# Tying hand-ordered operations of a decoder-layer kernel to one another, with weight splits behind bank copies in two attentions

## The chip, the cores and the metric

The kernel runs on one core of a Trainium2 chip. The metric is the device time in microseconds (us) of one execution; the time of a kernel is the median of its runs.

## The reference, cut to what matters

One decoder layer, in fp32: sequence length 1024, model width 1024, feed-forward width 2816, 256 memory tokens.

```python
def reference(x, mem, ...):
    h = rms_norm(x, norm1_g)
    p_rwkv, p_sb, q_mem, gate_logits = jnp.split(h @ w_in, cut, axis=-1)
    y_a = rwkv7_branch(p_rwkv, ...)                 # 8 heads of 64, a recurrence over time
    y_b = stick_breaking_branch(p_sb, ...)          # 8 heads of 64, causal, QK-norm
    y_m = memory_branch(q_mem, mem, ...)            # 4 heads of 128 into 256 memory tokens
    gates = jax.nn.sigmoid(gate_logits.reshape(b, t, 3, 1024))
    branch_out = jnp.einsum('btnc,ncd->btnd', jnp.stack([y_a, y_b, y_m], 2), w_branch)
    x = x + jnp.sum(gates * branch_out, axis=2) @ w_out
    return x + conv_ffn(rms_norm(x, norm2_g), w_up, conv_w, conv_b, w_down)

def stick_breaking_attention(q, k, v):              # by blocks of 128 queries
    z = q @ k.T * scale
    log_1mb = jnp.where(mask, log_sigmoid(-z), 0.0)
    log_between = reverse_cumsum(log_1mb) - log_1mb
    return jnp.where(mask, jnp.exp(log_sigmoid(z) + log_between), 0.0) @ v
```

## The kernel before

**Arithmetic.** A large fp32 product is done as three products on numbers that are split into a high part and a low part: high by high, high by low, low by high (`mm3`). A weight tile of 128x1024 is loaded through SyncE's DMA queue (`load_w`, L77) into one of two raw buffers and split by `split_raw`: ScalarE writes the high part (L81), then GpSimd the low part, raw minus high (L82). Each of the two has two buffers. `mmul` (L113) issues every product, `transpose` (L106) every transpose, both on TensorE.

**Banks.** The accumulators are eight PSUM banks of 128x512: four named `mm`, for the projections, and four named `g`, for all the rest. A projection piece needs two `mm` banks, which the function that ends it (`fin`) copies out: L755 for a branch gate (the sigmoid comes later, in `close`), L777 for the keys and L806 for the queries of stick-breaking, all on ScalarE; L1035 and L1036 on ScalarE and L1037 on VectorE for the memory's queries.

**Stages, in the order of the source.** (1) Startup. (2) `rwkv_prep`, four head pairs. (3) `sb_attn`, stick-breaking: 64 units, each of one head and 128 queries; a unit makes scores with a sigmoid, a scan on VectorE (L854), transposes with copies on ScalarE (`mid`, L866; the sigmoid is L848), and products with the values. (4) `mem_attn`, eight units. (5) `stage2`, the recurrence over 16 chunks, with ScalarE copies L538 and L550 and a VectorE update L530 in each; `norm_part` brings the group norm's squares (L580) between the chunks. (6) `group_norm`. (7) `branch_last` and `out_proj`. (8) `up_phase`, in steps that end in a convolution; its last operation writes the tile `gall`. (9) `down_phase`: per step two operands are split, ScalarE's L1676 and L1677 and VectorE's L1678 and GpSimd's L1679 (`prep`), and early in it the weights' sums are made (`t_sums`, L1655 and L1656). At the end of each pair of the up projection `act_sums` adds four tiles on VectorE (L1490).

**Two streams.** Projections run as a list of items, each a generator cut into pieces (eight per projection, one per 128 rows of the input); `pump` steps through them. `weave(main, pump, ratio)` takes one step of a stage and then `ratio` pieces of projection. In `sb_attn` the ratio is 1.03, in `mem_attn` 1.6, in `stage2` 2.08. `need(name)` runs pieces until an item has set the mark `name`: a head pair's queries and keys (`sb0` to `sb3`), the memory's keys and values (`kv`), a memory head's queries. The items beside stick-breaking are its later keys and queries with gates, then the memory's keys and values (`mv` and `mk`, eight short items of two or three pieces), then the memory's queries. `load_y` (L1118 loads, L1129 is its split on ScalarE) and `branch_item` (L1165 stores partial sums to `mrd`) run beside the recurrence.

**Who sets the order.** Instructions are written down in the order of the source, and a scheduler then orders each engine's queue by priority and its own estimate of when operands are ready, so that an operation may be moved ahead of one written earlier. `self.pinned(ins)` fixes an operation, while `self.pin` is set (from the end of startup to the group norm's end, in `branch_last`, for the last tile of the output projection, in the up projection and from the fourth step of the down projection): `keep_in_program_order` puts it behind the operation that was written immediately before it on the same engine, fixed or not. If that one slips, the fixed one may slip with it, past operations that were fixed earlier. Products, transposes and the attentions' copies and scans are fixed; the weight split (L81, L82) and the bank copies L755, L777 and L806 are not.

Of the kernel before, what the change touches and what calls it, by code (L numbers as in the profile page):

```python
# [12 lines left out]
F32 = mybir.dt.float32  # L13
F32R = mybir.dt.float32r
BF16 = mybir.dt.bfloat16
AF = mybir.ActivationFunctionType
ALU = mybir.AluOpType
# [33 lines left out]
class Trunk:  # L51
    def __init__(self, ctx, tc, I, out):
        self.ctx, self.tc, self.nc, self.I, self.out = ctx, tc, tc.nc, I, out
        self.uid = 0
        self.pin = False

    def nm(self, s):
        self.uid += 1
# [19 lines left out]
        return raw  # L78

    def split_raw(self, raw, hi, lo):  # L80
        self.nc.scalar.activation(hi, raw, AF.Copy)  # L81
        self.nc.gpsimd.tensor_tensor(lo, raw, hi.bitcast(F32), ALU.subtract)  # L82
        return hi, lo

    def split_w(self, src):
# [22 lines left out]
    def pinned(self, ins):  # L108
        if self.pin:
            self.tc.keep_in_program_order(ins)  # L110

    def mmul(self, *a, **k):
        self.pinned(self.nc.tensor.matmul(*a, **k))  # L113
# [635 lines left out]
    def gate_item(self, b, d, hook={}, keep=None):  # L749
        nc = self.nc  # L750

        def fin(pp):
            g = self.t4()
            for h in range(2):
                nc.scalar.activation(g[:, h * 512 : (h + 1) * 512], pp[h], AF.Copy)  # L755
            nc.vector.tensor_tensor(g, g, self.rbc, ALU.mult)  # L756

            def close():
                self.pinned(nc.scalar.activation(g, g, AF.Sigmoid))
                if keep is None:  # L760
                    nc.scalar.dma_start(self.gsd[b, d], g)
                else:
                    keep["g", d] = g

            self.open_gates.append(close)

        return self.proj_item(self.I["w_in"][30 + b * 8 + d], fin, hook)

    def sb_qk(self, p, out):
        nc = self.nc  # L770
        st = {}
        lo64, hi64 = slice(0, 64), slice(64, 128)

        def k_fin(pp):
            kr, sq = self.t4(), self.t4()
            for h in range(2):
                nc.scalar.activation(kr[:, h * 512 : (h + 1) * 512], pp[h], AF.Copy)  # L777
            nc.scalar.activation(sq, kr, AF.Square)
            st["k"] = sq, kr

        def k_ss():
            st["ex"] = self.expand_heads(self.head_norm(self.head_ss(st["k"][0]), 2, SBD, 1.0))

        def k_bc():
            kr = st["k"][1]
            bc = self.bcast_heads(st["ex"])
            for h in range(2):
                hs = slice(h * 512, (h + 1) * 512)
                nc.vector.scalar_tensor_tensor(kr[:, hs], kr[:, hs], self.par("sbk"), bc[h], ALU.mult, ALU.mult)
            st["K"] = [], []  # L790

        def k_split(i):
            kr = st["k"][1]
            K, KL = st["K"]
            for x in (K, KL):
                x.append(self.t4("qk", F32R))
            q, o = (lo64, hi64) if i == 0 else (hi64, lo64)
            nc.scalar.activation(K[i][q], kr[q], AF.Copy)
            nc.scalar.activation(K[i][o], kr[q], AF.Copy)
            nc.vector.tensor_tensor(KL[i][q], kr[q], K[i][q].bitcast(F32), ALU.subtract)  # L800
            nc.vector.tensor_tensor(KL[i][o], kr[q], K[i][q].bitcast(F32), ALU.subtract)

        def q_fin(pp):
            qr, sq = self.t4(), self.t4()
            for h in range(2):
                nc.scalar.activation(qr[:, h * 512 : (h + 1) * 512], pp[h], AF.Copy)  # L806
            nc.scalar.activation(sq, qr, AF.Square)
            st["q"] = sq, qr

        def q_split(i):  # L810
            qr = st["q"][1]
            st.setdefault("S", []).append(self.t4("qk", F32R))
            S = st["S"][i]
            q, o = (lo64, hi64) if i == 0 else (hi64, lo64)
            g = self.par("sbq")[q]
            nc.scalar.activation(S[q], qr[q], AF.Copy, scale=g)
            nc.vector.scalar_tensor_tensor(S[o], qr[q], g, S[q].bitcast(F32), ALU.mult, ALU.subtract)  # L817
            if i == 1:
                out.extend((st["S"], *st["K"], st["f"]))

        def q_ss():
            nf = self.small("nf", [128, 16])
            st["f"] = self.head_norm(self.head_ss(st["q"][0]), 2, SBD, SBD ** -0.5, nf)

        w = self.I["w_in"]
        hooks = {1: lambda: k_split(1), 3: q_ss, 4: lambda: q_split(0), 6: lambda: q_split(1)}
        kq = {4: k_bc, 5: lambda: k_split(0)}
        return self.proj_item(w[18 + p], k_fin), k_ss, self.proj_item(w[14 + p], q_fin, kq), hooks

    def sb_attn(self, qk, need):  # L830
# [952 lines left out]
    def run(self):  # L1783
        nc, tc = self.nc, self.tc
# [44 lines left out]
        def pumped():  # L1829
            due = 0  # L1830
            for _ in self.stream(items):
                due += pace[0]
                while due >= 10:
                    due -= 10
                    next(inv, None)
                yield

        pump = pumped()

        def need(name):  # L1840
            while name not in marks:
                next(pump)
# [2 lines left out]
            self.weave(self.rwkv_prep(p, krv[p], need), pump, 1.0)  # L1845
        pace[0] = 8
        need("sb0")
        self.weave(self.sb_attn(qk, need), pump, 1.03, 0)
        need("kv")
        self.weave(self.mem_attn(mq, need), pump, 1.6, 0)  # L1850
        need("mem")
        st2 = self.stage2()
        next(st2)
        need("y1")
# [83 lines left out]
```

## Time and profile before

| | |
|---|---|
| runs | 1835.12, 1835.45, 1835.46 us; median 1835.45 us |
| profiled execution | 1834.23 us, its span from first to last instruction 1832.5 us |
| mean granted TensorE clock | 0.997 |
| TensorE busy | 1783.7 us of the span |
| stick-breaking, 334 to 648 us | TensorE 308.36, VectorE 252.89, ScalarE 189.05, GpSimd 90.18 us busy |
| memory attention, 689 to 767 us | TensorE 76.82, VectorE 31.18, ScalarE 44.80, GpSimd 17.80 us busy |
| recurrence, 810 to 1014 us | TensorE 196.94 us busy, clock 0.98 |
| up projection, 1190 to 1613 us | TensorE 416.61, VectorE 323.01 us busy |
| down projection, 1613 to 1832 us | TensorE 211.38, VectorE 153.01 us busy |

All these are of one profiled execution, the runs apart. A busy time counts instructions under way on that engine. In rows of the timeline the columns are start, duration, engine, line, operation, output and inputs with their shapes, how many instructions the row holds, and in brackets the idle time before it and what ended that. In rows of the waits: who waited, for whom, total, times, longest. In rows of the windows: from and to, length, then the busy time and number of instructions of TensorE, its weight loads, VectorE, ScalarE and GpSimd, the granted TensorE clock as a share of full speed, the share of the DMA engines and GB/s. PE is TensorE, DVE is VectorE, ACT ScalarE, POOL GpSimd, SP SyncE.

### The profile page before, as it was taken

What the parts mean: (1) busy time and instruction counts of PE and PEld (TensorE: products, weight loads), DVE (VectorE), ACT (ScalarE), POOL (GpSimd) and SP (SyncE); (2) the same over time, 40 slices, a digit from 0 to 9 for tenths busy, and PEclk for the clock granted to TensorE, in tenths of its full rate; (3) what the DMA queues carried; (4) which work ended last, traced back from release to release, by engine and by line L of the source; (5) the groups of instructions that cost most, each with busy time, mean ns of one, the idle gap of its engine ahead of it and who ended that gap; (6) DMA issues with size and microseconds to landing.
All of it is one profiled execution on the core that took longest, in us unless ns stands there. A gap on an engine that the chain in (4) does not pass through costs nothing.

```text
span 1832.5 us, 27438 instructions
## 1 busy us (share of the span) xinstructions
PE 1783.7 (97%) x10468; PEld 1442.8 (79%) x10468; DVE 1185.4 (65%) x1659; ACT 881.4 (48%) x1665; POOL 770.6 (42%) x441
## 2 busy tenths in 40 slices
PE   8999999999999999999899999989999999999999
PEld 6777778778788887787777878868888888878877
DVE  5657664988987514333534792597776777794596
ACT  5443342564666636534456533454444444444333
POOL 2322343232222452122233350476767767635454
PEclk9999999999999999999999999999999999999999
DMA  4155466111112342467665563323332323395475
GB/s 181 58 172 184 161 195 198 50 41 52 56 50 81 111 143 55 167 212 256 229 230 185 194 220 104 127 68 106 113 106 87 119 95 116 115 334 206 138 248 189
DMA packets 120614, 263.39 MB, mean 144 GB/s; under 512 B 28314, under 2 KB 40858, under 8 KB 120355
## 3 DMA queue, kind: packets, MB, share of 16 engines
q1 hardware_dynamic: 82722, 194.76, 32.3%
q10 hardware_dynamic: 33984, 54.27, 8.1%
q0 software_dynamic: 3776, 12.62, 2.2%
q8 instruction: 82, 1.34, 0.3%
q14 instruction: 50, 0.40, 0.1%
HBM read 180.04 MB, written 81.53 MB: 143 GB/s over the span
## 4 chain that ended last, share of the span: by engine, by line
PE 81%; DVE 10%; issue 4%; ACT 2%; POOL 2%; DMA 1%; ACTq 0%; SPq 0%; DVEq 0%; POOLq 0%
PE mm L113 65%; PE g L113 13%; PE g L106 3%; POOL dw L1679 1%; DVE at L854 1%; DVE it L462 1%; DVE qk L379 1%; DVE qk L381 1%; DVE inst L464 1%; DVE BT L1318 1%; DVE mg L1232 0%; DVE qk L817 0%; DMA at<-scr 0%; DVE g L1474 0%; ACT wh L81 0%
## 5 line engine op out<-in xcount | busy, mean ns | idle before, releaser
L82 POOL TENSOR_TENSOR wl<-wr,wh 128x1024 fp32r<-128x1024 f32 x77 | 196.5, 2552 | 475.0 <-ACT wh L81 464.1
L113 PE MATMUL mm<-xhi,wh 128*128 128x512 f32 x784 | 263.3, 416 | 10.1 <-ACT xhi L182 8.1
L113 PE MATMUL mm<-xlo,wh 128*128 128x512 f32 x784 | 244.7, 393 | 0.3 <-DVE xlo L183 0.3
L113 PE MATMUL mm<-xhi,wl 128*128 128x512 f32 x784 | 243.2, 392 | 0.7 <-POOL wl L82 0.7
L113 PEld LDWEIGHTS mm<-xhi,wl 128*128 128x128 f32 x784 | 147.6, 188 | 34.3 <-POOL wl L82 1.6
L113 PEld LDWEIGHTS mm<-xlo,wh 128*128 128x128 f32 x784 | 147.9, 189 | 33.8 <-DVE xlo L183 1.0
L113 PEld LDWEIGHTS mm<-xhi,wh 128*128 128x128 f32 x784 | 137.2, 190 | 40.1 <-issue 9.1
L81 ACT ACTIVATE wh<-wr 128x1024 fp32r<-128x1024 f32 x77 | 81.4, 1057 | 143.6 <-PE mm L113 87.3
L113 PE MATMUL mm<-dw,da 128*128 128x512 f32 x528 | 121.5, 390 | 2.2 <-DVE da L1678 2.0
L113 PEld LDWEIGHTS mm<-dw,da 128*128 128x128 f32 x528 | 98.8, 188 | 24.3 <-DVE da L1678 3.4
L113 PE MATMUL mm<-BT,l 128*128 128x512 f32 x504 | 117.7, 389 | 0.0
L1679 POOL TENSOR_TENSOR dw<-draw,dw 128x512 fp32r<-128x512 f32 x55 | 81.5, 1488 | 83.3 <-ACT dw L1677 83.2
L113 PE MATMUL mm<-BT,wh 128*128 128x512 f32 x352 | 109.2, 390 | 2.8 <-DVE BT L1318 2.8
L854 DVE TENSOR_TENSOR_SCAN at<-at,at 128x128 f32<-128x128 f32 (+3 forms) x64 | 93.3, 1459 | 26.6 <-ACT at L848 26.4
L113 PEld LDWEIGHTS mm<-BT,l 128*128 128x128 f32 x504 | 94.6, 188 | 19.6
L113 PE MATMUL mm<-B,wh 128*128 128x512 f32 x352 | 108.6, 390 | 1.5 <-DVE p L1508 1.5
L1678 DVE TENSOR_TENSOR da<-draw,da 128x512 fp32r<-128x512 f32 x77 | 65.7, 863 | 57.6 <-ACT da L1676 57.1
L113 PE MATMUL g<-dw,da 128*128 128x512 f32 x396 | 90.9, 390 | 2.1 <-POOL dw L1679 1.1
L1409 POOL TENSOR_TENSOR l<-it,l 128x1024 fp32r<-128x1024 f32 x21 | 51.6, 2459 | 95.5 <-ACT l L1408 95.5
L113 PEld LDWEIGHTS g<-dw,da 128*128 128x128 f32 x396 | 74.2, 188 | 18.3 <-ACT dw L1677 1.4
L1676 ACT ACTIVATE da<-draw 128x512 fp32r<-128x512 f32 x77 | 48.3, 629 | 83.6 <-PE mm L113 38.1
L756 DVE TENSOR_TENSOR w<-w,rbc 128x1024 f32<-128x1024 f32 x24 | 49.8, 2074 | 56.8 <-ACT w L755 55.0
(329 smaller groups left out, 3989.9 us busy)
## 6 DMA issues: line engine op xcount, KB each, us to landing
wr<-in_w_in_dram SPq DMA_DIRECT2D x50, 512.0 KB, 3.7
draw<-actd SPq DMA_DIRECT2D x77, 256.0 KB, 4.3
at<-scr SPq DMA_DIRECT2D x28, 512.0 KB, 6.1
draw<-in_w_down_dram SPq DMA_DIRECT2D x55, 256.0 KB, 4.9
rw<-in_w_up_dram SPq DMA_DIRECT2D x22, 512.0 KB, 3.5
actd<-gall ACTq DMA_DIRECT2D x44, 256.0 KB, 3.4
gsd<-w ACTq DMA_DIRECT2D x20, 512.0 KB, 2.8
wr<-in_w_up_dram SPq DMA_DIRECT2D x20, 512.0 KB, 3.7
```

Source lines behind the costliest of these rows:

```text
L81: self.nc.scalar.activation(hi, raw, AF.Copy)
L82: self.nc.gpsimd.tensor_tensor(lo, raw, hi.bitcast(F32), ALU.subtract)
L106: self.pinned(self.nc.tensor.transpose(out, in_, self.ident[:n, :n]))
L113: self.pinned(self.nc.tensor.matmul(*a, **k))
L379: nc.vector.tensor_tensor(bk4[q, :, first ^ h2], self.c8(x[q, hs]), self.c8(Q[q, hs]), ALU.mult)
L381: nc.vector.scalar_tensor_tensor(ra4[:, :, 1, 1:64], self.c8(P[:, hs])[:, :, 0:63], -1.0, self.c8(kk[:, hs])[:, :, 1:64], ALU.mult, ALU.mult)
L756: nc.vector.tensor_tensor(g, g, self.rbc, ALU.mult)
L854: self.pinned(nc.vector.tensor_tensor_scan(sn[:, :W][:, ::-1], sn[:, :W][:, ::-1], self.smask[:, 1024 - W :][:, ::-1], 1.0, ALU.mult, ALU. ...
L1409: keep(eng.tensor_tensor(lo, src, hi.bitcast(F32), ALU.subtract))
L1676: self.pinned(nc.scalar.activation(A[:, 0], a, AF.Copy))
L1678: self.pinned(nc.vector.tensor_tensor(A[:, 1], a, A[:, 0].bitcast(F32), ALU.subtract))
L1679: nc.gpsimd.tensor_tensor(Wt[:, 1], w, Wt[:, 0].bitcast(F32), ALU.subtract)
```

## The change

Four edits. First, `pinned` now also ties an operation to the last one that was fixed on the same engine, wherever that was (`last_pinned` is kept for the whole kernel and is never reset); the tie is an order in the queue, without a semaphore. Second, the bank copies L755, L777 and L806 are fixed. Third, a flag `pin_split` fixes both halves of the weight split, and it is set from the start of `sb_attn` to the end of `mem_attn`. Fourth, three pieces of projection run ahead of `sb_attn`, after the first head pair's mark is set; the list of items stays the same, and both versions are through the same pieces when `sb_attn` ends.

```diff
     def __init__(self, ctx, tc, I, out):
-        self.pin = False
+        self.pin = self.pin_split = False
+        self.last_pinned = {}
...
     def split_raw(self, raw, hi, lo):
-        self.nc.scalar.activation(hi, raw, AF.Copy)
-        self.nc.gpsimd.tensor_tensor(lo, raw, hi.bitcast(F32), ALU.subtract)
+        keep = self.pinned if self.pin_split else lambda ins: None
+        keep(self.nc.scalar.activation(hi, raw, AF.Copy))
+        keep(self.nc.gpsimd.tensor_tensor(lo, raw, hi.bitcast(F32), ALU.subtract))
         return hi, lo
...
     def pinned(self, ins):
         if self.pin:
             self.tc.keep_in_program_order(ins)
+            last = self.last_pinned.get(ins.ins.engine)
+            if last:
+                self.tc.add_manual_dep(
+                    ins.ins, last, mybir.DependencyInfo(mybir.DependencyClass.NoSync, mybir.DependencyReason.DATA), reason="order")
+            self.last_pinned[ins.ins.engine] = ins.ins.name
+        return ins
...
         def fin(pp):                        # gate_item; k_fin and q_fin of sb_qk likewise
-                nc.scalar.activation(g[:, h * 512 : (h + 1) * 512], pp[h], AF.Copy)
+                self.pinned(nc.scalar.activation(g[:, h * 512 : (h + 1) * 512], pp[h], AF.Copy))
...
         need("sb0")
+        self.pin_split = True
+        for _ in range(3):
+            next(pump)
         self.weave(self.sb_attn(qk, need), pump, 1.03, 0)
         need("kv")
         self.weave(self.mem_attn(mq, need), pump, 1.6, 0)
         need("mem")
+        self.pin_split = False
         st2 = self.stage2()
```

More of the change, by code (lines that the diff above doesn't have):

```diff
@@ L776, in k_fin @@
             for h in range(2):
-                nc.scalar.activation(kr[:, h * 512 : (h + 1) * 512], pp[h], AF.Copy)
+                self.pinned(nc.scalar.activation(kr[:, h * 512 : (h + 1) * 512], pp[h], AF.Copy))
             nc.scalar.activation(sq, kr, AF.Square)
@@ L805, in q_fin @@
             for h in range(2):
-                nc.scalar.activation(qr[:, h * 512 : (h + 1) * 512], pp[h], AF.Copy)
+                self.pinned(nc.scalar.activation(qr[:, h * 512 : (h + 1) * 512], pp[h], AF.Copy))
             nc.scalar.activation(sq, qr, AF.Square)
```

## The prediction

> **What bounds the kernel.** I read the page first, its busy times and the chain; then the waits, restricted to TensorE from 310 to 1020 us; then the timeline of each engine at the places where TensorE waits; last the windows, for the granted clock.
>
> ```profile
> PE 1783.7 (97%) x10468; PEld 1442.8 (79%) x10468; DVE 1185.4 (65%) x1659; ACT 881.4 (48%) x1665; POOL 770.6 (42%) x441
> ```
>
> TensorE is busy for 1783.7 of 1832.5 us. The change gives it no product less and no product more: it changes the order in which three engines are served and when three pieces of projection run. So it can move only the 48.8 us in which TensorE stands still, plus the time that it runs at a lower clock after standing still. The waits of both attentions and of the recurrence behind them, longest in total first (columns: who waited for whom, total us, times, longest):
>
> ```profile
> PE g L113 <- DVE ys L530: 3.8, 2, 3.0
> PE g L113 <- ACT qk L550: 3.3, 3, 1.8
> PE g L106 <- DVE at L854: 2.2, 2, 1.5
> PE mm L113 <- DVE qk L1037: 1.2, 1, 1.2
> PE g L106 <- DVE hn L701: 1.1, 1, 1.1
> PE g L113 <- DVE hn L701: 0.9, 1, 0.9
> PE mm L113 <- ACT w L755: 0.8, 1, 0.8
> PE mm L113 <- ACT w L806: 0.7, 1, 0.7
> ```
>
> These are all the waits of that stretch, 14 us. L530 and L550 belong to the recurrence, the other six (6.9 us) to the two attentions. The six are the most that the part of the change named in its title can win.
>
> **Part a: three pieces ahead of stick-breaking.**
>
> ```profile
> 343.44 0.33 PE L106 MATMUL g<-kon,at 128*128 128x128 f32 x1 [1.52 <-DVE at L854]
> ```
> ```profile
> 345.85 3.34 PE mm L113 x18
> ```
>
> The first unit's transposes wait 1.52 us for its scan (L854), which hangs on the queries' factors and not on TensorE. Three pieces are 18 products of 512 columns; the chain shows 18 in 3.34 us. Put ahead of the first unit they fill the 1.52 us and more: **-1.5**. They are taken from pieces that had to be run in a burst when the second head pair's mark was not yet set, so later the order of pieces and units is the same within a step. Between 0 and -1.5; I take the end, since 3.34 is over twice the wait.
>
> **Part b: weight splits behind the bank copies.**
>
> ```profile
> 387.92 1.06 ACT L81 ACTIVATE wh<-wr 128x1024 fp32r<-128x1024 f32 x1 [0.25 <-issue]
> 388.88 1.06 ACT L806 ACTIVATE w<-mm 128x512 f32<-128x512 f32 x2
> ```
>
> The split's first half (L81, 1.06 us) runs on ScalarE ahead of the two copies that empty the projection's banks (L806), and TensorE's next product waits 0.7 for such a bank. The wait of 0.8 on L755 and that of 1.2 on L1037 (the memory queries' banks) have the same L81 ahead of the same kind of copy. With the copies first each copy is ready 1.06 earlier: the 0.8 and all but 0.1 of the 1.2 go. The 0.7 goes too, but what is late next lies close:
>
> ```profile
> 390.00:400.00 10.00, 10.00 (x87) 8.13 (x86) 9.94 (x7) 7.38 (x14) 2.13 (x1) 1.00 0.25 67
> ```
> ```profile
> 402.26 1.19 PE L113 MATMUL g<-qk,qk 128*128 128x512 f32 x4 [0.86 <-DVE hn L701]
> ```
>
> VectorE is busy for 9.94 of these 10 us, and 12 us later TensorE waits for it anyway. A TensorE that is 0.7 earlier waits 0.5 longer there, so I count 0.2 of it. Together **-2.1**, between 0 (all swallowed) and -2.7.
>
> **Part c: what the later splits cost.** A fixed split stands behind whatever the source has ahead of it on ScalarE, the attention's copies too. In the long items (48 products) a split has many us to spare; in the eight short ones of the memory's keys and values it has not:
>
> ```profile
> 631.72 1.07 ACT L81 ACTIVATE wh<-wr 128x1024 fp32r<-128x1024 f32 x1 [0.46 <-issue]
> 632.69 1.24 ACT L848 ACTIVATE at<-g,nf 128x512 f32<-128x512 f32 x2
> 633.83 0.87 ACT L866 ACTIVATE at<-g 128x512 f32<-128x512 f32 x2
> ```
> ```profile
> 632.88 2.39 POOL L82 TENSOR_TENSOR wl<-wr,wh 128x1024 fp32r<-128x1024 f32 x1 [2.06 <-ACT wh L81]
> ```
> ```profile
> 637.93 0.28 PE L113 MATMUL mm<-qk,wl 128*128 128x256 f32 x1
> ```
>
> L848 and L866 are written ahead of this L81. Behind them it starts at 634.70 at the earliest instead of 631.72, 2.98 later; the GpSimd half (L82) ends at 638.25 instead of 635.27, and the first product that reads it stands at 637.93: late by 0.3. Queued behind the fixed split are later attention copies, but its own input is there, so it holds them for its 1.07 us alone. On SyncE the next weight load (L77) waits for L82 and goes 3 us later, with one item to spare. Four of eight at 0.3: **+1.2**, from 0 to +2.4 (all eight). Nothing below 0, since no product waits less for a later split.
>
> **Part d: the tie on ScalarE in the recurrence.** The tie puts every fixed operation behind the fixed one before it, in the whole kernel. Before, an operation was fixed only behind its immediate predecessor, so it could slip with it past earlier fixed ones.
>
> ```profile
> 871.48 0.33 PE L113 MATMUL g<-ys,at 64*64 64x64 f32 x4 [1.76 <-ACT qk L550]
> 872.63 0.33 PE L113 MATMUL g<-ys,at 64*64 64x64 f32 x4 [0.81 <-ACT qk L550]
> ```
> ```profile
> 871.00:877.00 6.00, 4.70 (x33) 3.79 (x34) 2.03 (x6) 1.83 (x11) 2.93 (x1) 0.72 0.65 233
> 893.00:899.00 6.00, 5.83 (x46) 4.52 (x48) 1.30 (x6) 2.80 (x9) 0.00 (x0) 0.72 0.79 288
> 1628.90:1634.90 6.00, 6.00 (x26) 4.98 (x27) 5.83 (x6) 1.85 (x4) 2.58 (x2) 1.00 0.94 328
> ```
>
> Here squares of the group norm (L580) and a branch split (L1129), which the source has behind the eight copies L550, run among them; TensorE waits 2.57 us for the copies' banks, and then runs at a granted clock of 0.72 for 6 us, which costs (1 - 0.72) x 6 = 1.7. With the tie both go, 4.3 us. But 20 us later stands the wait of 3.0 on L530, and what is ahead of that is a load that waits for a store:
>
> ```profile
> SPq L1118 <- DMA mrd<-w: 6.4, 1, 6.4
> ```
>
> This load does not follow TensorE, so an earlier TensorE mostly waits longer there. Between 0 (all swallowed) and -4.3; I take **-1.8**, a little nearer to the swallowing end.
>
> The Trainium skill (TensorE: Matmul & The Clock Gate, What's actually happening) says that the clock falls to half after an idle window of about 3.4 us, whose phase is free. By it alone neither the 2.57 nor the 3.0 need have lowered the clock, and part d could be worth 2.6 at most; the trace has 0.72 behind both, so the measurement decides.
>
> **Part e: the tie on VectorE between the up and the down projection.** This is where the change works against itself.
>
> ```profile
> 1609.81 0.68 DVE L1655 TENSOR_TENSOR dT<-u 128x512 f32<-128x512 f32 x1
> ...
> 1620.29 1.43 DVE L1678 TENSOR_TENSOR da<-draw,da 128x512 fp32r<-128x512 f32 x1
> 1621.64 0.68 DVE L1490 TENSOR_TENSOR gall<-gall 128x512 f32<-128x512 f32 x1
> 1622.24 0.68 DVE L1678 TENSOR_TENSOR da<-draw,da 128x512 fp32r<-128x512 f32 x1
> 1622.84 2.98 DVE L1490 TENSOR_TENSOR gall<-gall 128x512 f32<-128x512 f32 x3
> 1625.75 0.68 DVE L1655 TENSOR_TENSOR dT<-u 128x512 f32<-128x512 f32 x1
> ```
> ```profile
> 1612.96 14.59 PE L113 MATMUL mm<-dw,da 128*128 128x512 f32 x62
> 1628.89 11.40 PE L113 MATMUL mm<-dw,da 128*128 128x512 f32 x49 [1.35 <-DVE da L1678]
> ```
>
> The four L1490 end the up projection; the source has them ahead of the first weight sums (L1655 and L1656) and of the operand splits L1678 of down steps 3 and 4. All are fixed. On the chip L1655 ran at 1609.81 and both L1678 at 1620.29 and 1622.24, ahead of L1490s. The tie forbids that: after the conv ends at 1620.29 come four L1490, L1655, L1656, and only then step 3's L1678. Before, six operations took from 1620.29 to 1625.75; now a seventh, 0.68, has to pass: step 3's operand is ready at 1626.4. TensorE does 62 products in 14.59 us, 0.235 each, twelve a step, and a step's third product needs that operand: step 3's is due at 1612.96 + 38 x 0.235 = 1621.9. It waits 4.5 us. From there to step 5's third product are 24 products, 5.6 us: 1632.0, where it started at 1628.89 before. That is +3.1, since the old wait of 1.35 is swallowed; and a wait of 4.5, longer than the 3.0 behind which the clock was 0.72, costs 1.7 more (behind 1.35 it stayed 1.00). Together **+4.8**. From +0.7 (only the seventh operation counts) to +6.2 (4.5 and 1.7, nothing swallowed). TensorE stays the bound to the end, so the loss isn't given back.
>
> The Trainium skill (SBUF — State Buffer, SBUF: two separate sides) says that a vector operation with two inputs in SBUF and a GpSimd operation exclude each other for their whole length. By it the 2.98 for three L1490 is GpSimd's doing; freed from it seven operations at 0.68 would be done at 1625.1, and the sum of this part +3.5.
>
> **Sum.** -1.5 - 2.1 + 1.2 - 1.8 + 4.8 = +0.6. The profiled execution took 1834.23 (span 1832.5 and 1.7 around it); the median of the runs is 1835.45, 1.2 above. 1834.23 + 0.6 = 1834.8 as a profile, **1836.1** as a median. A difference of 0.2% is 3.7 us, about what a measurement can tell from none.
>
> **Rivals.** *Slower: a bank copy as a plug in the recurrence.* The gates' bank copy L755 is fixed there as well, so every fixed copy of the recurrence behind it (L538, L550) must wait while it waits for a free buffer to write to. For it:
>
> ```profile
> 890.63 1.08 ACT L755 ACTIVATE w<-mm 128x512 f32<-128x512 f32 x2 [1.34 <-DMA qk<-vd]
> ```
>
> this copy did wait, just ahead of the 3.0. Against it: the other waits are not behind L755. One such plug costs what that one does, 3.0 + 1.7 = 4.7, and decides once the copy's buffer comes later than TensorE's next visit to the recurrence. Sum 1836.1 + 4.7 = 1840.8.
>
> *Faster: the recurrence keeps its gain and the vector queue hardly loses.* Part d at -4.3 and part e at +0.7, if the conv's last operations move up where the weight sums ran: 1836.1 - 2.5 - 4.1 = 1829.5. Against it: VectorE is without a gap from 1620.29 to 1625.75, and the L1490 need the conv's last results.
>
> *The tie does nothing:* parts d and e fall away, 1836.1 + 1.8 - 4.8 = 1833.1, still within 0.2%. Against it: each tied pair above is out of source order in the trace, so an order that holds must show.
>
> **Chances.** Forecast 0.43, the tie without effect 0.05, slower 0.31, faster 0.21. The first two are within 0.2%: 0.48. The low end reaches to the faster case, the high end past the slower one by a clock's price: 1829.5 to 1842; the likeliest case alone runs from 1832 to 1839.
>
> **What would show it.** Right: no TensorE wait near the first scan; L81 behind L755, L806 and L1036 in both attentions; L550 in one block ahead of L580; L1490 x4 ahead of L1655 and L1678 near 1620, and a new TensorE wait of about 4.5 on L1678 with a clock below 1 behind it. Wrong: no wait at the start of the down projection (then faster); waits of over 0.5 on L82 in the memory's short items, or a second wait of 3 in the recurrence (then slower).

## The result, and the profile after

The change makes the kernel slower: 1855.76 us against 1835.45, ratio 1.0101 with a 95% interval of 1.0089 to 1.0114. The forecast was 1836.1, with a range from 1829.5 to 1842. The profiled execution took 1856.85 (span 1855.1, before 1832.5). The medians and ratios of the experiments below are of their fast executions: one or two of e1, e5, e6, e7 and e8 took from 2963 to 8415 us and are left out (with them the median of e5 is the 1844.4 that an expectation below names).

Lines behind the edited ones have moved by 2 to 8 in the changed file: L1677 is L1685, L1490 is L1498, L866 is L874, L82 is L84.

The page's busy times of the changed kernel, and its waits over the whole span (who waited for whom, total, times, longest):

```profile
PE 1797.1 (97%) x10468; PEld 1452.8 (78%) x10468; DVE 1186.8 (64%) x1659; ACT 882.1 (48%) x1665; POOL 772.8 (42%) x441
```
```profile
PE mm L121 <- ACT dw L1685: 7.7, 1, 7.7
...
PE g L121 <- DVE ys L538: 4.4, 2, 3.5
PE mm L121 <- POOL wl L84: 2.9, 2, 1.9
...
PE g L108 <- DVE at L862: 2.5, 2, 2.0
...
PE mm L121 <- ACT w L814: 1.8, 1, 1.8
PE g L121 <- ACT qk L558: 1.7, 2, 1.4
PE g L108 <- ACT at L874: 1.6, 1, 1.6
```

TensorE has the same 10468 products and is busy for 13.4 us longer, and it stands still for 9.2 us longer (58.0 against 48.8). Most of the longer busy time is the granted clock: TensorE was busy for 31.8 us at half clock, for 10.1 before, and half of that difference is 10.9 of the 13.4. In the windows (columns as before; the clock is the third number from the end) it is 0.50 at places where it was 1.00 before, since the kernel before has half clock at 269, 873 and 894 us and at its end alone:

```profile
476.50:479.90 3.40, 3.40 (x11) 2.63 (x10) 3.37 (x4) 3.37 (x5) 0.76 (x1) 0.50 0.00 0
664.20:667.60 3.40, 3.40 (x17) 3.40 (x17) 0.00 (x0) 0.09 (x1) 2.14 (x1) 0.50 0.69 204
1637.00:1647.20 10.20, 4.46 (x10) 3.18 (x11) 5.73 (x5) 4.38 (x8) 5.00 (x4) 0.50 0.76 286
```

Counting TensorE's products in both traces shows where the lag arises. It is the start of the n-th product after, less that before:

| product | start before | lag after | what lies between |
|---|---|---|---|
| 1800 | 339.1 | +4.0 | startup and preparation |
| 3600 | 609.2 | +9.3 | stick-breaking but for its end |
| 4800 | 800.0 | +13.4 | memory's short items, memory attention |
| 6900 | 1014.4 | +11.5 | recurrence |
| 9300 | 1557.4 | +13.2 | output and up projection |
| 9900 | 1695.7 | +22.1 | turn from the up to the down projection |
| 10467 | 1828.3 | +22.6 | down projection |

So there are three losses: 5.3 in stick-breaking, 4.1 at the memory's items, 8.9 at the turn to the down projection. The recurrence gains 1.9. The 1.7 between 6900 and 9300 is one half clock at 1105 us, behind a wait of 1.5 on L1228 that the kernel before has as well. The first 4.0 lie ahead of stick-breaking; the last experiment below returns to them.

The largest first. TensorE, then VectorE, ScalarE and SyncE's queue at that turn, from the timeline of the changed kernel:

```profile
1626.16 8.32 PE L121 MATMUL mm<-dw,da 128*128 128x512 f32 x36
1642.18 0.79 PE L121 MATMUL mm<-dw,da 128*128 128x512 f32 x1 [7.70 <-ACT dw L1685]
```
```profile
1633.61 2.62 DVE L1498 TENSOR_TENSOR gall<-gall 128x512 f32<-128x512 f32 x4
1636.14 0.68 DVE L1663 TENSOR_TENSOR dT<-u 128x512 f32<-128x512 f32 x1
1636.86 0.69 DVE L1664 TENSOR_TENSOR dT<-wr,dT 128x512 f32<-128x512 f32 x1
1640.86 0.69 DVE L1686 TENSOR_TENSOR da<-draw,da 128x512 fp32r<-128x512 f32 x1 [3.31 <-ACT da L1684]
```
```profile
1629.18 4.16 ACTq L1503 DMA_DIRECT2D actd<-gall  x3
1635.65 0.39 ACTq L1508 DMA_DIRECT2D actd<-gall  x1
1636.26 0.33 ACTq L1507 DMA_DIRECT2D actd<-gall  x1
1640.20 0.63 ACT L1684 ACTIVATE da<-draw 128x512 fp32r<-128x512 f32 x1 [12.15 <-DMA draw<-actd]
1641.50 0.63 ACT L1685 ACTIVATE dw<-draw 128x512 fp32r<-128x512 f32 x1 [0.67 <-DMA draw<-in_w_down_dram]
```
```profile
1635.19 0.33 SPq L1674 DMA_DIRECT2D draw<-actd  x1
```

The kernel before had the load and the first copy of step 3 here:

```profile
1609.39 0.38 SPq L1666 DMA_DIRECT2D draw<-actd  x1
1614.06 0.63 ACT L1676 ACTIVATE da<-draw 128x512 fp32r<-128x512 f32 x1 [0.70 <-DMA draw<-actd]
```

VectorE's queue has the order that was foreseen: four sums L1498, L1663, L1664, then the split L1686 of step 3. But VectorE is not what is late; it waits 3.31 itself. Step 3's tile is loaded only at 1635.19. In the kernel before it was loaded at 1609.39 and its two ScalarE copies ran from 1614.06; on this trace's time, 13.2 later, that is 1622.6 and 1627.3. Here ScalarE issues the five stores of the up projection's last tiles and sums first, idles, and copies at 1640.20. The stores delay the load as well. SyncE's queue stands still for the last 2.4 us ahead of 1635.19, until the first of ScalarE's stores has landed (waits of SyncE's queue, 1610 to 1645 us):

```profile
SPq L1674 <- DMA actd<-gall: 2.4, 1, 2.4
```

### The profile page after: what moved, and what is told of

Read it like the earlier page. It is cut to its first block, busy times and chain, and to the rows that moved or that the text cites. A ratio compares the mean times of both kernels' runs of the same rounds, so it can differ in the third digit from the quotient of the medians.

```text
span 1855.1 us, 27432 instructions
## 1 busy us (share of the span) xinstructions
PE 1797.1 (97%) x10468; PEld 1452.8 (78%) x10468; DVE 1186.8 (64%) x1659; ACT 882.1 (48%) x1665; POOL 772.8 (42%) x441
## 4 chain that ended last, share of the span: by engine, by line
PE 63%; issue 3%; DVE 3%; POOL 2%; DMA 1%; ACT 1%; ACTq 0%; SPq 0%; POOLq 0%; DVEq 0%
PE mm L121 53%; PE g L121 9%; PE g L108 2%; POOL dw L1687 1%; DVE BT L1326 1%; POOL wl L84 0%; DMA w<-yd 0%; DMA mrd<-w 0%; DMA actd<-gall 0%; DMA draw<-in_w_down_dram 0%; DVE g L1482 0%; DVE qk L597 0%; DVE g L1483 0%; ACT wh L83 0%; DVE keep L1706 0%
## 5 line engine op out<-in xcount | busy, mean ns | idle before, releaser
L84 POOL TENSOR_TENSOR wl<-wr,wh 128x1024 fp32r<-128x1024 f32 x77 | 198.3, 2575 | 452.9 <-ACT wh L83 428.8
L121 PEld LDWEIGHTS mm<-BT,l 128*128 128x128 f32 x504 | 94.6, 188 | 19.6
L1686 DVE TENSOR_TENSOR da<-draw,da 128x512 fp32r<-128x512 f32 x77 | 64.8, 849 | 66.2 <-ACT da L1684 65.6
L177 POOL TENSOR_TENSOR hf<-rs,half 128x16 f32<-128x16 f32 (+1 forms) x18 | 48.5, 2694 | 105.8 <-DVE rs L174 101.2
```

The lines of the kernel that those rows point to most:

```text
L84: keep(self.nc.gpsimd.tensor_tensor(lo, raw, hi.bitcast(F32), ALU.subtract))
L177: nc.gpsimd.tensor_tensor(out, t[:, :n], self.half[:, :n], ALU.pow)
L1686: self.pinned(nc.vector.tensor_tensor(A[:, 1], a, A[:, 0].bitcast(F32), ALU.subtract))
```

## The experiments

The medians, each beside the kernel before on the same chip:

| kernel | median | before | ratio, 95% interval |
|---|---|---|---|
| e1, no tie | 1850.2 | 1836.48 | 1.0070, 1.0056 to 1.0084 |
| e2, tie only | 1844.38 | 1836.48 | 1.0042, 1.0029 to 1.0056 |
| e3, tie cut at the turn | 1843.98 | 1836.48 | 1.0036, 1.0022 to 1.0050 |
| e4, no pieces | 1847.19 | 1836.48 | 1.0051, 1.0039 to 1.0064 |
| e5, pieces only | 1843.65 | 1836.22 | 1.0036, 1.0026 to 1.0046 |
| e6, free splits | 1852.21 | 1836.22 | 1.0076, 1.0064 to 1.0088 |
| e7, bank copies and cut tie | 1834.14 | 1836.22 | 0.9983, 0.9974 to 0.9993 |
| e8, cut tie | 1833.24 | 1836.22 | 0.9983, 0.9973 to 0.9993 |
| e9, pieces paid back | 1840.08 | 1836.51 | 1.0023, 1.0013 to 1.0033 |
| e10, tie without VectorE | 1834.36 | 1836.51 | 0.9986, 0.9977 to 0.9995 |
| e11, long splits | 1832.63 | 1836.51 | 0.9978, 0.9969 to 0.9987 |

By these intervals a difference of two medians is known to about 2 us. The changed kernel itself was not run again beside the experiments.

**The tie.** Three kernels of the first session.

```diff
 # e1, from the change
-            last = self.last_pinned.get(ins.ins.engine)
-            if last:
-                self.tc.add_manual_dep(ins.ins, last, ...)
-            self.last_pinned[ins.ins.engine] = ins.ins.name
```


> The change without its tie (bank copies, weight splits and the three pieces stay). Theory A, the tie between the last up sums (L1498) and the first down splits costs the 8.9 us by which TensorE falls back between 1612 and 1700 us, and the tie helps the recurrence by 1.9: 1855.8 - 8.9 + 1.9 = 1849, no wait of 7.7 at the start of the down projection, the attentions as slow as with the change. Rival B, the tie makes the attentions slow as well, since a late fixed copy holds all later ones: about 1838, no half clock in the attentions.

```diff
 # e2, from the change: bank copies L763, L785, L814 not fixed, and
-        self.pin_split = True
-        for _ in range(3):
-            next(pump)
```


> The kernel before with the tie alone. Theory A: 1835.5 + 8.9 - 1.9 = 1842.5, the wait of 7.7 on L1685 with half clock behind it, the attentions as before. Rival B: the attentions lose too, 1850 or more. Rival C, the tie does nothing by itself and only the later arrival of TensorE matters: within 2 us of 1835.5.

```diff
 # e3, from the change, in down_phase
         for s in range(ahead):
             prep(s)
         self.pin = True
+        self.last_pinned = {}
```


> The change with the tie cut once, at the start of the fixed part of the down projection. Theory A: 1855.8 - 8.9 = 1846.9; step 3's load back in third place of the SyncE queue's down loads, its two ScalarE copies ahead of the stores of the last up sums, TensorE's wait there 1.4 as before. Rival C: the loss there stays, 1855.

All three came out by theory A: e1 1850.2 (1849 expected), e2 1844.4 (1842.5), e3 1844.0 (1846.9), each within 3 us. TensorE's wait at the turn, from the waits near 1605 to 1670 us, for e2 and then for e3, and ScalarE's timeline of e3:

```profile
PE mm L121 <- ACT dw L1685: 7.8, 1, 7.8
```
```profile
PE mm L121 <- DVE da L1686: 1.4, 1, 1.4
```
```profile
1625.76 0.63 ACT L1684 ACTIVATE da<-draw 128x512 fp32r<-128x512 f32 x1 [0.64 <-DMA draw<-actd]
1626.48 0.63 ACT L1685 ACTIVATE dw<-draw 128x512 fp32r<-128x512 f32 x1
...
1627.77 0.90 ACTq L1503 DMA_DIRECT2D actd<-gall  x2
```

One line that forgets the last fixed operation brings step 3's copies back ahead of the stores and the wait back to 1.4. Two more runs of the tie by itself say what it is worth where it does no harm, and whose it is:

```diff
 # e8, from e2: the cut of e3 in down_phase
+        self.last_pinned = {}
```


> The kernel before with the tie alone, cut at the down projection. Theory: of the tie alone (1844.4) the 10.5 us by which it falls back there go, less the 1.6 that it made up by 1700 us: 1835.5, with TensorE's idle time 2.6 below that of before up to the recurrence's end. Rival: the cut is worth 11.8 as in the change: 1832.6.

```diff
 # e10, from e2
-            if last:
+            if last and ins.ins.engine != self.nc.vector.engine:
```


> The kernel before with the tie on every engine but VectorE. Theory A: it is VectorE's tie (last up sums ahead of the first down splits) that costs the down projection its 10.5, and ScalarE's that helps the recurrence: no wait of 7.8, about 1834 as with the cut tie, or 1835.5 if the first scan's wait of 1.5 is back. Rival: ScalarE's tie holds the first down splits as well: 1840 or more.

e8 took 1833.24, 3.0 below the kernel before and nearer to the rival's 1832.6 than to the 1835.5 expected; the cut is thus worth 10.9 (7.9 + 3.0) in the kernel with the tie alone, and 12.8 in the change (20.3 - 7.5). e10 took 1834.36, with a wait of 1.3 at the turn. So the harm comes from VectorE's tie, and the gain from the ties of the other engines. With step 3's split on VectorE held behind the last sums, the scheduler put step 3's load behind four more loads of later steps in SyncE's queue: it is the seventh load of L1674 there instead of the third, and the third again in e3. That this follows from the scheduler's estimate of when operands are ready is likely, but no run shows it. Tying one engine's queue has reordered two others. Whether the late load or ScalarE's five stores ahead of the copies weighs more was not tried apart; in the trace the load lands last, and it waits for one of the stores. The gain is in the recurrence, where the copies L558 now stand in one block (eight from 867.12 to 869.00 in e8); the wait for them was 3.3 and that for L530 3.8 (waits of e8 from 860 to 1020 us):

```profile
PE g L121 <- DVE ys L538: 2.9, 2, 1.9
PE g L121 <- ACT qk L558: 1.6, 2, 1.2
```

**The three pieces.**

```diff
 # e4, from the change
-        for _ in range(3):
-            next(pump)
```


> The change without the three pieces ahead of stick-breaking. Theory A, the pieces gain the 1.5 of the first scan: 1857, the wait of 1.5 on the first scan back, the other waits of the attentions as with the change. Rival D, the pieces shift the projection against the units and so cause the waits at 376 (1.95), 412 (1.63) and 474 (1.76 and a half clock): 1850, these three waits gone.

```diff
 # e5, from the kernel before
         need("sb0")
+        for _ in range(3):
+            next(pump)
```


> The kernel before with the three pieces alone. Theory D, the pieces by themselves shift the vector work of the projections onto the scans of the first units: without them the change took 8.6 us less, of which the first scan's 1.5 is set off here, so 1836.5 + 8.6 - 1.5 = 1843.6, with waits near 376, 412 and 474. Rival E, they do harm only together with the fixed splits and copies: 1835, the first scan's wait of 1.5 gone and no new one.

Theory D, which was no part of the forecast, holds. Without the pieces the change is at 1847.19 (1850 expected by it), 10.7 above the kernel before instead of 20.3, and the three waits are gone. The pieces alone cost 7.4 (1843.65; 1843.6 expected). The waits of e5 from 334 to 500 us, and ScalarE at the longest of them:

```profile
PE mm L113 <- ACT at L866: 3.1, 3, 1.3
PE g L106 <- ACT at L866: 2.1, 1, 2.1
```
```profile
409.05 1.06 ACT L81 ACTIVATE wh<-wr 128x1024 fp32r<-128x1024 f32 x1 [0.93 <-issue]
410.02 0.58 ACT L755 ACTIVATE w<-mm 128x512 f32<-128x512 f32 x1
410.62 1.14 ACT L816 ACTIVATE qk<-w,params 64x1024 fp32r<-64x1024 f32 x1
411.79 0.77 ACT L866 ACTIVATE at<-g 128x512 f32<-128x512 f32 x2
```

A weight split, a bank copy and a query split, 2.7 us of the projection's ScalarE work, stand just ahead of the attention's copy L866 for which TensorE waits 2.1. That the lead of three pieces puts them there was tested by giving the lead back at once:

```diff
 # e9, from e5
-    def weave(self, main, filler, ratio, off=300):
-        acc = 0.0
+    def weave(self, main, filler, ratio, off=300, acc=0.0):
...
-        self.weave(self.sb_attn(qk, need), pump, 1.03, 0)
+        self.weave(self.sb_attn(qk, need), pump, 1.03, 0, -3.0)
```


> The kernel before with the three pieces ahead of stick-breaking, and the first three pieces of the weave left out in return, so that from the third step on pieces and units meet as before. Theory D: the harm of the pieces (1844.4 against 1836.2) is the lead of three pieces that the first 16 units keep: it goes, the first scan's wait of 1.5 stays away, 1834.7, and the waits at 389 to 479 are the 0.7, 0.9, 0.8 and 1.1 of before. Rival: the burst itself does the harm (banks and weight buffers taken too early): 1840 or more.

Half of it held. The waits of the kernel before on L701, L755 and L806 are back to the tenth (e9, 330 to 500 us), but the sum missed, 1840.08 against 1834.7, and is the rival's. Most of the miss is in the first of these rows:

```profile
PE g L106 <- DVE at L854: 4.1, 2, 3.3
PE g L106 <- DVE hn L701: 1.1, 1, 1.1
...
```

The rival blamed banks and weight buffers that are taken too early; VectorE's timeline shows another cause, first in e9, then in the kernel before:

```profile
341.94 2.96 DVE L462 TENSOR_TENSOR it<-inst 128x720 f32<-128x720 f32 x1
...
345.76 1.00 DVE L854 TENSOR_TENSOR_SCAN at<-at,at 128x128 f32<-128x128 f32 x2
```
```profile
340.79 2.60 DVE L854 TENSOR_TENSOR_SCAN at<-at,at 128x128 f32<-128x128 f32 x1
```

The pieces bring other work with them: for every ten pieces the kernel also writes down eight steps of a matrix inversion on VectorE (L462 and L464 in turn, all fixed). Three pieces ahead of the first unit put two of these steps ahead of its scan, where they followed it before. TensorE comes to the transposes at 342.89 in e9, 1.0 later than before, but the scan starts 5.0 later; the wait is 3.3 instead of 1.5, and TensorE ran at half clock behind it.

**The splits and the bank copies.**

```diff
 # e6, from the change
-        self.pin_split = True
```


> The change with the weight splits left free (bank copies, pieces and tie stay). Theory F, a fixed split behind the attention's copies is late in the short items of the memory's keys and values: the waits of 0.95 and 1.92 on GpSimd's half and the half clock behind them go, 3.8 us, the waits at 376, 412 and 474 stay: 1852. Rival E, the fixed splits also make those three: 1846 or less.

```diff
 # e7, from the change: no pieces, no pin_split, and the cut of e3
-        self.pin_split = True
-        for _ in range(3):
-            next(pump)
...
+        self.last_pinned = {}
```


> The kernel before with the fixed bank copies and the tie cut at the down projection; no fixed splits, no pieces. Theory: TensorE's idle time in stick-breaking falls by 3.5 (as in the change without its pieces, up to 610 us) and in the recurrence by 0.6 to 0.8, nothing is lost in the memory's items nor at the down projection: 1836.5 - 4.2 = 1832.3, give or take one half clock of 1.7. Rival: the 1.7 between 1.8 and 3.5 were the splits' doing, and the bank copies bring nothing: 1834.

```diff
 # e11, from e7: pin_split set ahead of sb_attn; in mv and mk of mem_kv
+    def free_split(self, src):
+        keep, self.pin_split = self.pin_split, False
+        w = self.split_w(src)
+        self.pin_split = keep
+        return w
```


> The cut tie with the fixed bank copies and fixed weight splits, but the splits of the memory's eight short items left free, and no pieces ahead. Theory F: it keeps what the change without its pieces had gained up to 610 us (idle time 1.3 below that of the cut tie alone) and loses nothing in the short items: 1833.9 - 1.3 = 1832.6, no wait on GpSimd's half at 632 and 650. Rival: the gain is given back where VectorE is full (the wait of 1.55 near 401): 1834.

e6 came at 1852.21 (1852 expected): with the splits free, the waits on GpSimd's half (2.9 us in the row above) are gone, and the time is 4.3 us lower (20.3 - 16.0). Between TensorE's 3600th and 4200th products, in the short items, e6 falls back by 0.1 against the kernel before, the change by 4.9. e7 missed its expectation of 1832.3: it took 1834.14, within 1 us of e8 without fixed bank copies. The order of TensorE's queue is the same in both, and so are the waits of 0.8 and 0.7 on the copies (e8, 330 to 770 us, copies L763 and L814; e7 has them too):

```profile
PE mm L121 <- ACT w L763: 0.8, 1, 0.8
...
PE mm L121 <- ACT w L814: 0.7, 1, 0.7
```

Fixing the copies moves nothing as long as the free split may pass them. e11, which fixes both but leaves the eight short items alone, came at 1832.63 as expected (1832.6). Its interval overlaps that of e8; the waits tell them apart, 4.0 us from 330 to 770 us against 5.5, and the one on GpSimd is 0.6 (the lines of e11 behind its `free_split` have moved by 6 more):

```profile
PE g L127 <- DVE hn L715: 1.5, 1, 1.5
PE g L114 <- DVE hn L715: 1.0, 1, 1.0
PE mm L127 <- POOL wl L84: 0.6, 1, 0.6
PE mm L127 <- DVE qk L1051: 0.5, 1, 0.5
PE mm L127 <- ACT w L820: 0.4, 1, 0.4
```

The wait of 1.5 on L715 is the one that was foreseen where VectorE is full; it takes back part of the gain. e11 is the fastest version: 3.9 us below the kernel before, ratio 0.9978 (e7, e8 and e10 are below it too, by 2 to 3 us). So the tie across the turn, the three pieces and the fixed splits of the short items are what makes the change slow: the first two cost when put in alone, the third costs 4.3 in the change (e6), and without all three the rest is faster than before.

**The kernel before once more.**

> The kernel before, unchanged, for a second profile. If half clock follows short waits and stretches of tiny products by the phase of a free-running window, some of its places differ from those of the first profile (266 us, 871, 893) at the same order and the same waits, and the time differs by multiples of 1.7; if it follows the waits alone, the places are the same.

It took 1836.52, span 1834.7. Up to stick-breaking the half clock is at other places (104, 155 and 312 us against 269), in the recurrence at the same two. The windows of this run, then the products ahead of the second one:

```profile
308.40:311.80 3.40, 3.40 (x71) 2.89 (x70) 1.04 (x3) 2.44 (x4) 1.33 (x1) 1.00 0.02 5
311.80:315.20 3.40, 3.40 (x9) 2.62 (x10) 2.84 (x4) 1.36 (x2) 2.60 (x2) 0.50 0.40 93
```
```profile
309.63 1.10 PE L113 MATMUL g<-kon,ys 8*64 8x4 f32 x32
310.66 1.10 PE L113 MATMUL g<-kon,w 128*64 128x2 f32 x32
```

The first profile of the same program had 1.00 there, behind the same tiny products, which ended at 310.0:

```profile
310.40:313.80 3.40, 3.40 (x17) 2.79 (x16) 2.53 (x4) 1.35 (x2) 2.61 (x2) 1.00 0.46 145
```

Of the fourteen profiles of this document, whose products are the same in that stretch, eleven have half clock between 308 and 316 us. And this run has no wait of 1.5 on the first scan: its only wait for L854 is one of 0.7 at 493 us. TensorE came to the first scan at 345.20 and found it done; in the first profile it came at 341.92 and waited until 343.44. The wait of 1.52 on which part a was built is what a run pays that comes early: without the half clock ahead of it, TensorE waits for the scan instead. The scan's own length is in the wait too: 2.60 us at 340.79, with GpSimd's L82 beside it (340.00 to 343.10), but 0.42 in the changed kernel at 348.01, with GpSimd idle. Half clocks are also most of the lag of 4.0 in the table: the changed kernel has three ahead of its 1800th product (104, 272 and 313 us), the first profile of the kernel before has one, and this run has three and is 3.2 behind that profile there.

## Why the prediction was wrong

The place of the largest loss and the tie that makes it were foreseen, the path by which it comes was not, and the second largest loss was booked as a gain. The parts against what the runs showed:

- **Part a, -1.5; measured +7.4 alone, +9.6 in the change.** The failed step is the sentence "later the order of pieces and units is the same within a step". Counted in the products of both traces, it holds from the 33rd unit on; for the first 16 units the projection runs three pieces ahead (two at the 8th and 9th), for the next 16 one, and its ScalarE and VectorE work falls on other units (e5, e9). And the 1.52 was no price at all, since a second run of the same kernel did without it. The part was bounded "between 0 and -1.5"; no end above nothing was given, and the range lacked over 7 us for it.
- **Part b, -2.1, and part c, +1.2; measured together +4.3.** One profile each of e4 and e2, which differ in the fixed splits and copies alone, tell them apart: e4 gains 1.7 on e2 between TensorE's 1800th and 3600th products and 0.9 in the memory attention, and loses 4.9 in the short items between. So part b is right where split and copy are both fixed (the waits of e11 against e8 agree), and so was the swallowing near 402 us. Part c's mechanism is right too, a late GpSimd half in the short items; its price of 0.3 each was the term that failed. The trace has one wait of 0.95 and one of 1.92, with half clock behind the second. ScalarE's timeline of the changed kernel ahead of that one shows why:

```profile
657.85 1.24 ACT L897 ACTIVATE ys<-mm,jk 64x128 f32<-64x128 f32 x4 [1.15 <-PE mm L121]
659.12 0.46 ACTq L900 DMA_DIRECT2D yd<-ys  x1
659.68 1.06 ACT L83 ACTIVATE wh<-wr 128x1024 fp32r<-128x1024 f32 x1 [0.60 <-ACT ys L897]
```

  The split was counted behind the copies' durations. It also stands behind their waits: four output copies that wait 1.15 for TensorE, and the issue of their store, 0.60 more.
- **Part d, -1.8.** Near: 3.0 and 2.2 less in e8 and e10, where the tie does no harm. The waits on the copies L558 fell as forecast. How much of that is swallowed was a choice between two ends: the wait on L538 is 2.9 in e8 and 4.4 in e10, 3.8 before.
- **Part e, +4.8 with an upper end of 6.2; measured +10.9 alone, +12.8 in the change.** The order on VectorE is the one that was written down, and four sums took even less than foreseen (2.62; the three of before took 2.98). GpSimd stood still beside them:

```profile
1642.20 6.36 POOL L1687 TENSOR_TENSOR dw<-draw,dw 128x512 fp32r<-128x512 f32 x4 [26.34 <-ACT dw L1685]
```

  By the Trainium skill (SBUF — State Buffer, SBUF: two separate sides) a VectorE operation with two inputs in SBUF and a GpSimd operation hold each other up; the trace agrees with it, 0.66 each alone. The failed step is that only VectorE's queue was followed. The operation that was tied has a load on SyncE and two copies on ScalarE ahead of it, and the scheduler moved these too. TensorE therefore stops at step 3's first product, for ScalarE's copy L1685, and not at its third for VectorE's split; the wait is 7.7 instead of 4.5, and the granted clock is 0.50 for 10.2 us about its end, three times the stretch that had been allowed.
- **The sum.** 7.9 for the tie (e2), 7.4 for the pieces (e5) and 4.3 for the splits (e6) make 19.6; measured are 20.3. With about 2 us of doubt in each the parts add up, so nothing large is left. Taken out of the change one at a time they are worth more, 12.8, 9.6 and 4.3, which make 26.7; from the change down to e11, which has none of the three, it is 24.2 (20.3 + 3.9), since what is left gains.
- **The rivals.** The slower one, a bank copy as a plug in the recurrence, did not come: the waits there are 4.4 and 1.7 on L538 and L558, and the recurrence gained. The tie that does nothing is refuted by e2. A slower case was given 0.31, for a wrong reason.
- **The signs.** The splits behind the bank copies, the copies of the recurrence in one block, the four sums ahead of L1655 and L1678, and no wait of 1.5 at the first scan all came as written. The last of these says nothing: e4, without the pieces, and the second run of the kernel before lack that wait too. The new wait near 1620 came, but on ScalarE's copy and not on L1678. And a sign that was listed for slower came, a wait of over 0.5 on L82 in the short items.

## What to carry to other kernels

Before tying an operation to an earlier one, follow back everything that exists only for it, its loads and copies on other engines' queues included: a scheduler that is told it may start later will start these later too. A tie that is never cut reaches across stages; cut it where one stage ends. Work that is pulled ahead of a stage is taken from somewhere: look at what it covered there, and at which later steps its tail now falls on. And take a second profile of the kernel before, before a wait of 1.5 us is put into a sum.

## What the runs showed of the hardware

The half clock came here without an idle TensorE. Two rows of tiny products, 64 in 2.1 us with the engine busy throughout (309.63 and 310.66 above), were followed by 3.4 us at 0.50. Short waits were followed by it too: 1.76 and 1.92 in the changed kernel (ahead of 476.5 and 664.2 above), though one of 1.95 that ended at 377.94 was not. And the same place has it in one run and not in the other: the second run of the kernel before is 1.7 behind the first at the 1600th product, ahead of that place, and 3.2 at the 1700th. The Trainium skill (TensorE: Matmul & The Clock Gate, What's actually happening) says that the clock is set by how busy the array was in a free-running window of about 3.4 us. The stretches here, 3.4 us and three times that, agree with it, and so does their change from run to run; an idle time of a whole window, which the same section of the Trainium skill gives as the condition for half clock, was not needed.
